# Second block of a two-block transformer: the projection products become one stream that is put out between the stages of the attention items

## The chip, the cores and the metric

The kernel runs on one core of a Trainium2 chip. All weights and activations are float32; every large matrix product is made as three products of "fp32r" parts (high by high, low by high, high by low). The metric is the device time of one execution in microseconds (us), and the less the better.

## The reference, cut to what matters

512 tokens of width 1024 pass through a first block (two layers of mixer and feed-forward network) and a second block. The change is in the second block, which computes:

```python
h = rmsnorm(x, attn_norm)
z = h @ w_in                                    # 3*512 columns dil, 3*512 columns fox, 8 forget gates
o_dil = dilated_attention(q_d, k_d, v_d, rel_bias)       # 8 heads of 64, causal, a bias by distance
log_f = log_sigmoid(z_forget + b_forget)
c = cumsum(log_f, axis=1)
s = q_f @ k_f.T * 64 ** -0.5 + c[t] - c[s]               # fox: 8 heads of 64, causal
o_fox = softmax(s) @ v_f
x = x + concat(rmsnorm(o_dil, g_dil), rmsnorm(o_fox, g_fox)) @ w_out
x = x + hierarchical_moe(rmsnorm(x, ffn_norm))           # 1 of 4 groups, 2 of its 8 experts
```

## The kernel before

Tokens stand in four tiles of 128. A weight "unit" of 2048 floats a partition is loaded into a `raw` tile (SyncE's queue), ScalarE (ACT) rounds it to `whi` (L147), VectorE (DVE) makes `wlo` (L148), and `mm3` (L171 to L173) issues the three products of one 128x512 piece. There are three buffers each of `raw`, `whi` and `wlo`. The order of instructions on each engine is chosen by a scheduler when the kernel is built; an engine then takes them strictly in that order.

Around the change the program runs so. The last feed-forward network of the first block ends with its down products; token tile by token tile follow the post norm, the residual and the pre norm of the second block (`rq`, `hn`), transposes on TensorE (L197) and copies to `acth` and `actl` (L201, L202): these are `h`. Then `second` runs:

1. `qkv` for dil: `nat_proj` makes `sv` (v, 96 products), then the forget product (24 products) and its chain in `forget` (DVE and ACT: exp, log, reciprocal, running sum, `fc` last), then q and k of all eight heads (192 products, kept as `sq`, `skh`, `skl`).
2. `attend` for dil: 16 items (4 pairs of heads by 4 query tiles), each with three stages that `staged` interleaves by `LAG = (0, 1, 2)`: `scores` (L1013, L1016, then `soft`: DVE adds the bias and takes the maximum at L882, POOL negates it at L883, ACT takes exp at L884), `turn` (transposes L893, copies `pt`), `values` (L913). After a pair's last tile `back` (L922) turns the output to tokens on partitions.
3. `out_norm` of dil: norm, transposes, copies to `mixd`.
4. the same for fox: 288 products, then 16 items with a mask product (L1019), and two decay products a pair (L1115), which read `fc`.
5. `tail`: `out_proj` with all of `w_out` (192 products, first the left 512 columns for the four tiles, then the right ones), and per tile the residual, norm and router. Then `moe`, whose 32 experts are read from memory.

`self.hold`, set from `HOLD_D` and `HOLD_F`, keeps the splitting of some later weights behind earlier instructions. The line numbers of the changed kernel are some two higher up to `back`, and its scores, masks, decay products stand at L1105 and L1111, L1108, L1160.

Of the kernel before, what the change touches and what calls it, by code (L numbers as in the profile page):

```python
# [22 lines left out]
P = 128  # L23
# [66 lines left out]
class Builder:  # L90
# [60 lines left out]
    def col_unit(self, w, c0, n=256):  # L151
        """w [1024, N]: all rows, n columns -> views [P, 8, n]"""
# [9 lines left out]
    def row_unit(self, w, r0, c0=0, n=1024, raw=None):  # L162
        """rows r0.. of w, n columns: [P, 2048/n, n]"""
# [25 lines left out]
    def to_T(self, src, tt, dst, kb0=0, n=None):  # L189
        """src [P tok, n*128] fp32 -> dst (hi, lo) tiles [:, kb0.., tt block]"""  # L190
# [14 lines left out]
    def mean_sq(self, ss, j, src, q=None):  # L205
        """ss[:, j] = sum(src ** 2) / D over half a row"""
# [127 lines left out]
    # ---- even mixer  # L334
    def even(self, h, mix):
# [17 lines left out]
        # v, tokens on partitions  # L353
# [22 lines left out]
        # masked, transposed token weights: wm[s, g, t], s <= t  # L376
# [7 lines left out]
        # a and u, transposed  # L384
# [103 lines left out]
    def nat_proj(self, w, c0, n, h):  # L488
        """h^T w[:, c0:c0+n] with tokens on partitions: four PSUM tiles"""
# [13 lines left out]
    def odd_tables(self):  # L503
        """rotary tables; kept for the odd mixer"""
# [14 lines left out]
    def odd_ret(self, h, mb):  # L519
        """retention, two heads at a time; returns what is left to emit"""  # L520
# [10 lines left out]
        def two(c0, c1):  # L531
            """columns c0..c0+255 and c1..c1+255 side by side, tokens on partitions"""
# [101 lines left out]
    def nsa(self, np_, cp, h, mixp, mid):  # L634
# [15 lines left out]
        def rope(pool, n, a, b, tt):  # L650
            """rotates the first 16 columns of each 64 in n viewed [P, a, b, 64]"""
# [11 lines left out]
        # kc | vc | ks | vs  # L663
# [23 lines left out]
        # kw | vw | gates  # L687
# [15 lines left out]
        # compressed keys and values  # L703
# [22 lines left out]
        # q: head b and head b + 4 share a block of 128 rows  # L726
# [87 lines left out]
        def selected(qt, br, b):  # L814
            """heads b and b + 4 over the selected keys (br 0) or the window's (br 1)"""
# [56 lines left out]
    def soft(self, pool, s, bias, nk, acc):  # L872
        """one head, one tile of queries: scores in PSUM (plus bias from SBUF) -> exp(s - max), the sums into acc"""
# [14 lines left out]
    def keys_first(self, pool, e, nk, odd):  # L888
        """e [queries, keys] -> keys on partitions, block by block"""
# [11 lines left out]
    def staged(self, items, lag=LAG):  # L901
        """items' stages interleaved: an item's stage k is put out lag[k] items after its first"""
# [6 lines left out]
    def pair_av(self, av, et, qt, v):  # L909
        """v^T e of two heads, one in each half of av's rows"""  # L910
# [5 lines left out]
    def back(self, pool, av, tag):  # L916
        """av, features on partitions -> tokens on partitions, block by block, in PSUM"""
# [50 lines left out]
    def qkv(self, pool, w, c0, h, between=None):  # L968
        nc = self.nc
        q = self.t(pool, "sq", [P, 8, T], F32R)  # L970
        kh = self.t(pool, "skh", [P, 8, T], F32R)
        kl = self.t(pool, "skl", [P, 4, T], F32R)
        v = self.t(pool, "sv", [P, NT, 512])
        pv = self.nat_proj(w, c0 + 1024, 512, h)
        for tt in range(NT):
            nc.scalar.activation(v[:, tt, :], pv[tt], AF.Copy)
        if between:
            between()
        for which in range(2):
            for b in range(2):  # L980
                u = self.col_unit(w, c0 + which * 512 + b * 256)
                for f in range(2):
                    p = self.ps()
                    for k in range(KD):
                        self.mm3(p, [z[:, k, f * P:(f + 1) * P] for z in u], [z[:, k, :] for z in h], k == 0,
                                 k == KD - 1)
                    for i in range(2):
                        hd = 4 * b + 2 * f + i
# [735 lines left out]
```

## Time and profile before

| | us |
|---|---|
| three timed runs | 1931.82, 1935.98, 1929.04 (median 1931.82) |
| the profiled execution, span from its first to its last instruction | 1934.0 |
| TensorE busy with products | 1866.0 (96 %) |
| TensorE busy loading weights | 1485.9 (77 %) |
| DVE, ACT, POOL busy | 1075.0, 789.2, 165.9 |
| mean granted TensorE clock | 0.971 of full speed |

The profiled execution is known by its span alone, and that is its own time here; it lies 2.2 us above the median of the timed runs. Products overlap in TensorE's pipeline, so a row's duration is longer than the distance to the next start: the starts tell the rate.

### The profile page before, as it was taken

How to read it: one execution, taken by the hardware profiler on the slowest of the kernel's cores; microseconds unless marked ns; L12 is line 12 of the kernel's file. 1: busy time of each engine (PE TensorE's matmuls, PEld its weight loads, DVE VectorE, ACT ScalarE, POOL GpSimd, SP SyncE). 2: the span in 40 equal slices, each digit the busy share in tenths (PEclk: the TensorE clock that was granted, in tenths of full speed). 3: DMA queues.
4: the chain of work that ended last, by engine and by line, in shares of the span. 5: the costliest groups of instructions: out<-in, count | busy, mean ns of one | idle time of the engine just before them, and what ended most of it. 6: DMA issues, size and time to landing. Idle time of an engine off the chain costs nothing.

```text
span 1934.0 us, 24404 instructions
## 1 busy us (share of the span) xinstructions
PE 1866.0 (96%) x9690; PEld 1485.9 (77%) x9691; DVE 1075.0 (56%) x1677; ACT 789.2 (41%) x1282; POOL 165.9 (9%) x303
## 2 busy tenths in 40 slices
PE   8999999999999989999999999999999979999997
PEld 6778888888899777678888888776686767676774
DVE  7654535444753444645444445663524477788876
ACT  6343222222422434644222222444536337666664
POOL 1010000000332100011000000200201240000000
PEclk9999999999999996999999999997998979999999
DMA  7433232323331210053233232240211408899994
GB/s 226 142 131 131 88 109 88 109 87 107 122 97 47 87 44 1 1 174 109 87 97 100 89 108 88 88 147 15 90 61 50 145 1 284 305 328 301 314 315 186
DMA packets 178326, 246.56 MB, mean 127 GB/s; under 512 B 10838, under 2 KB 144886, under 8 KB 178082
## 3 DMA queue, kind: packets, MB, share of 16 engines
q1 hardware_dynamic: 168352, 230.31, 36.0%
q10 hardware_dynamic: 9858, 14.67, 2.3%
q8 instruction: 77, 1.26, 0.3%
q14 instruction: 39, 0.32, 0.1%
HBM read 238.65 MB, written 8.93 MB: 128 GB/s over the span
## 4 chain that ended last, share of the span: by engine, by line
PE 29%; issue 19%; DVE 3%; POOL 2%; ACT 2%; POOLq 0%; ACTq 0%; DVEq 0%
PE mm L1408 6%; PE mm L1429 3%; PE px L1447 3%; PE px L1248 3%; PE mm L172 3%; PE mm L173 3%; PE mm L171 3%; PE px L913 2%; PE tp L893 1%; PE mm L1013 1%; PE mm L1016 1%; POOL rq L213 0%; DVE wlo L148 0%; ACT whi L147 0%; PE tp L1372 0%
## 5 line engine op out<-in xcount | busy, mean ns | idle before, releaser
L148 DVE TENSOR_TENSOR wlo<-raw,whi 128x2048 fp32r<-128x2048 f32 (+2 forms) x175 | 397.1, 2271 | 296.0 <-ACT whi L147 295.5
L147 ACT ACTIVATE whi<-raw 128x2048 fp32r<-128x2048 f32 (+2 forms) x175 | 331.6, 1897 | 476.1 <-issue 198.2
L171 PE MATMUL mm<-acth,whi 128*128 128x512 f32 (+2 forms) x968 | 365.6, 378 | 0.0
L172 PE MATMUL mm<-actl,whi 128*128 128x512 f32 (+2 forms) x968 | 364.7, 377 | 0.0
L173 PE MATMUL mm<-acth,wlo 128*128 128x512 f32 (+2 forms) x968 | 364.3, 376 | 0.0
L172 PEld LDWEIGHTS mm<-actl,whi 128*128 128x128 f32 (+1 forms) x968 | 181.9, 188 | 34.5 <-issue 1.0
L171 PEld LDWEIGHTS mm<-acth,whi 128*128 128x128 f32 (+1 forms) x968 | 181.9, 188 | 34.2 <-issue 0.7
L173 PEld LDWEIGHTS mm<-acth,wlo 128*128 128x128 f32 (+1 forms) x968 | 181.8, 188 | 34.2 <-issue 0.2
L171 PE MATMUL mm<-whi,acth 128*128 128x256 f32 (+2 forms) x480 | 159.9, 335 | 2.1 <-ACT gate L693 1.7
L172 PE MATMUL mm<-wlo,acth 128*128 128x256 f32 (+2 forms) x480 | 158.1, 330 | 0.6 <-DVE wlo L148 0.6
L173 PE MATMUL mm<-whi,actl 128*128 128x256 f32 (+2 forms) x448 | 145.4, 326 | 0.4 <-DVE actl L202 0.3
L317 DVE TENSOR_TENSOR macc<-px,macc 128x512 f32<-128x512 f32 x144 | 97.7, 689 | 75.2 <-PE px L173 75.2
L171 PE MATMUL px<-whi,hidh 128*128 128x512 f32 x352 | 137.5, 391 | 0.6 <-DVE macc L317 0.6
L173 PE MATMUL px<-whi,hidl 128*128 128x512 f32 x352 | 137.9, 392 | 0.0
L172 PE MATMUL px<-wlo,hidh 128*128 128x512 f32 x352 | 137.4, 390 | 0.0
L1408 PE MATMUL mm<-wlo,hg 128*128 128x512 f32 x256 | 102.3, 403 | 2.1 <-DVE wlo L148 2.1
L1408 PE MATMUL mm<-whi,hg 128*128 128x512 f32 x256 | 102.5, 401 | 0.0
L171 PEld LDWEIGHTS mm<-whi,acth 128*128 128x128 f32 x480 | 91.5, 191 | 11.1 <-ACT gate L693 1.9
L172 PEld LDWEIGHTS mm<-wlo,acth 128*128 128x128 f32 x480 | 91.4, 191 | 8.7 <-DVE wlo L148 1.5
L173 PEld LDWEIGHTS mm<-whi,actl 128*128 128x128 f32 x448 | 85.4, 191 | 6.9 <-DVE actl L202 1.0
L297 DVE TENSOR_TENSOR hidf<-mm,silu 128x512 f32<-128x512 f32 x44 | 30.4, 691 | 94.8 <-PE mm L173 94.8
L171 PEld LDWEIGHTS px<-whi,hidh 128*128 128x128 f32 x352 | 66.1, 188 | 16.3 <-DVE macc L317 1.5
(408 smaller groups left out, 2816.8 us busy)
## 6 DMA issues: line engine op xcount, KB each, us to landing
raw<-in_w_expert_gate SPq DMA_DIRECT2D x64, 512.0 KB, 5.7
raw<-in_w_expert_up SPq DMA_DIRECT2D x64, 512.0 KB, 8.4
actl<-in_w_expert_down SPq DMA_DIRECT2D x30, 1024.0 KB, 7.1
raw<-in_ffn_w_gate SPq DMA_DIRECT2D x22, 1024.0 KB, 5.3
raw<-in_ffn_w_up SPq DMA_DIRECT2D x22, 1024.0 KB, 5.3
raw<-in_ffn_w_down SPq DMA_DIRECT2D x22, 1024.0 KB, 4.8
raw<-in_od_w_in SPq DMA_DIRECT2D x12, 1024.0 KB, 5.1
raw<-in_w_in SPq DMA_DIRECT2D x12, 1024.0 KB, 5.3
```

Of the source, the lines that this page charges most:

```text
L147: self.nc.scalar.activation(hi[:, :n], raw[:, :n], AF.Copy)
L148: self.nc.vector.tensor_tensor(lo[:, :n], raw[:, :n], hi[:, :n].bitcast(F32), op=ALU.subtract)
L171: mm(out, l[0], r[0], start=first, stop=False)
L172: mm(out, l[0], r[1], start=False, stop=False)
L173: mm(out, l[1], r[0], start=False, stop=last)
L297: nc.vector.tensor_tensor(hf, pu[f], s, op=ALU.mult)
L317: nc.vector.tensor_tensor(m, p, m, op=ALU.add)
L913: self.nc.tensor.matmul(av[64 * i:64 * i + 64], v(i, kb), et[i][:, kb * P:(kb + 1) * P], start=kb == 0, stop=kb == qt)
L1248: self.nc.tensor.matmul(o, h2[i][:, tt, kb * P:(kb + 1) * P], s1[:, tt, :], start=tt == 0 and i == 0, stop=tt == NT - 1 and i == 1)
L1408: nc.tensor.matmul(ps, hg[kb][:, ee, :], hl[i][:, k, :], start=kb == 0 and i == 0, stop=kb == KD - 1 and i == 1)
L1429: nc.tensor.matmul(dn[hf][64 * e:64 * e + 64, :], heT[:, f * P + 64 * e:f * P + 64 * e + 64], rv[e][:, f, hf * 512:(hf + 1) * 512], start= ...
L1447: nc.tensor.matmul(p, ST[i][:, tt * P:(tt + 1) * P], z, start=n == 0, stop=n == 3)
```

## The change

The projection products are written as pieces, each a generator that gives up control after three products (a "chunk"): v of dil (32 chunks), four pairs of dil (16 each: q and k of two heads), v of fox, pair 0 of fox, forget (8), pairs 1 to 3 of fox, and then the first half of the output projection (rows 0 to 511 of `w_out`, 32 chunks, added to `x`). The 32 items of both attentions are one list. TensorE's order is kept as written there (`manual_schedule`): v of dil and pair 0, then per slot `scores(n)`, `values(n-2)`, `turn(n-1)`, late pieces (`back`, the dil norm), and 7 chunks (5 from slot 16 on). Other engines' order is still chosen by the scheduler. The PSUM pools are closed and opened anew twice (`psum`): at the start of `second` and at the start of `tail`. `tail` keeps only rows 512 to 1023 of `w_out` (`second_out`, 96 products, tile by tile). The holds go; `x` moves to the tile of `actl`, the experts' down weights to that of `mixd`; a pair's weights are loaded by two transfers instead of a unit by one.

```diff
-HOLD_N, HOLD_D, HOLD_F = 8, 8, 8
+HOLD_N = 8
+QUOTA = (7, 5)
...
-    def qkv(self, pool, w, c0, h, between=None):
...
+    def pair_unit(self, w, c0):
+        raw = self.load_unit([(j * 1024, KD, P, w[:, c0 + 512 * j:c0 + 512 * j + P].rearrange("(k p) n -> p k n", p=P))
+                              for j in range(2)])
+        return [z.rearrange("p (w k n) -> p w k n", w=2, k=KD) for z in self.split_w(raw)]
+    def pair_piece(self, pool, w, c0, b, h, sets):
...
+            for which in range(2):
+                p = self.ps()
+                for k in range(KD):
+                    self.mm3(p, [z[:, which, k, :] for z in u], [z[:, k, :] for z in h], k == 0, k == KD - 1)
+                    if k < KD - 1:
+                        yield
...
+    @staticmethod
+    def stream(pieces):
+        ready = pieces[0][0]()
+        for n, (_, run) in enumerate(pieces):
+            now = ready
+            ready = pieces[n + 1][0]() if n + 1 < len(pieces) else None
+            yield from run(now)
...
-    def second(self, h, src=None):
+    def second(self, h, src):
...
+        self.psum(mm=3, sc=2, tp=2, px=1)
...
-        dq = self.qkv(qp, w, 0, h, lambda: fg.extend(self.forget(qp, w, h)))
...
-        self.attend(at, dq, toep, False, o)
-        out_norm(o, "out_norm_dil_2", mix[0])
-        self.hold = self.marks[-HOLD_D]
-        fq = self.qkv(qp, w, 1536, h)
-        self.hold = ()
...
+        dense = self.stream([self.value_piece(qp, w, 1024, h, vals[0])] + [pair(0, b) for b in range(4)]
+                            + [self.value_piece(qp, w, 2560, h, vals[1]), pair(1, 0), self.forget_piece(qp, w, h, fg)]
+                            + [pair(1, b) for b in range(1, 4)]
+                            + [(lambda: None, lambda _: room()), self.half_out_piece(A["w_out_2"][0], mix[0])])
...
+        until(lambda: vals[0] and sets[0])
...
+        with self.tc.manual_schedule(engines={mybir.EngineType.PE}):
+            for n in range(len(items) + 2):
+                if n < len(items):
...
+                    until(lambda: len(sets[a]) > b and (a == 0 or fg))
+                    built[n] = self.item(at, b, qt, sets[a], vals[a], (toep, decay)[a], a == 1, o[a], S)
+                    built[n][0]()
+                if n >= 2:
...
+                    built[n - 2][2]()
...
+                if 1 <= n <= len(items):
+                    built[n - 1][1]()
+                for f in late.pop(n, []):
+                    f()
+                pull(QUOTA[n >= 16])
...
+        for tt in range(NT):
+            self.to_T(out_norm(tt, o[1], g), tt, mix[1])
...
-        self.out_proj(A["w_out_2"][0], mix, part, (normed, routed), (0, 1))
+        self.second_out(A["w_out_2"][0], mix, part, (normed, routed))
```

On TensorE, at the start of the second block, the order before puts v products (`mm`, of tiles 0 and 1) ahead of the transposes of token tile 2 (`tp` from `hn`); 24 of them stand there, and 20 more ahead of the transposes of tile 3:

```order
L173 MATMUL mm_9835<-whi_9818,actl_9580 128x512
L171 MATMUL mm_9835<-whi_9818,acth_9579 128x512
L172 MATMUL mm_9835<-wlo_9819,acth_9579 128x512
L173 MATMUL mm_9835<-whi_9818,actl_9580 128x512
L197 MATMUL tp_9745<-ident_72,hn_9735 128x128 x4
L197 MATMUL tp_9753<-ident_72,hn_9735 128x128 x4
L171 MATMUL mm_9822<-whi_9876,acth_9579 128x512
L171 MATMUL mm_9848<-whi_9818,acth_9579 128x512
```

In the changed kernel the same place reads:

```order
L173 MATMUL px_9705<-whi_9519,hidh_9397 128x512
L174 MATMUL px_9705<-wlo_9520,hidh_9397 128x512
L175 MATMUL px_9705<-whi_9519,hidl_9398 128x512
L199 MATMUL tp_9745<-ident_72,hn_9735 128x128 x4
L199 MATMUL tp_9753<-ident_72,hn_9735 128x128 x4
L199 MATMUL tp_9786<-ident_72,hn_9776 128x128 x4
L199 MATMUL tp_9794<-ident_72,hn_9776 128x128 x4
L173 MATMUL mm_9839<-whi_9821,acth_9579 128x512
```

The last down products (`px`) are followed by all 16 transposes of tiles 2 and 3, and no v product stands ahead of these any more.

On ACT, ahead of the first scores, the changed kernel puts the rounding of the third pair's weights (`whi_10169`, which takes the buffer that pair 0's products read) ahead of the copies of pair 0's keys (`skh`), which the first scores read; on DVE `wlo` and `skl` stand in the same order:

```order
L149 ACTIVATE whi_10016<-raw_10013 128x2048
L960 ACTIVATE sq_9950<-mm_9953 64x512 x2
L149 ACTIVATE whi_10169<-raw_10166 128x2048
L960 ACTIVATE skh_9951<-mm_9982 64x512
L963 ACTIVATE skh_9951<-mm_9982 64x512
L960 ACTIVATE skh_9951<-mm_9982 64x512
L963 ACTIVATE skh_9951<-mm_9982 64x512
```

In the kernel before all eight heads' keys are made ahead of the first scores, so pair 0's stand long ahead.

On DVE, at slots 13 to 15, the forget chain (`raw` 8x512, ending in `fc`) now stands among the soft maxima, copies and splits of the stream:

```order
L1045 RECIPROCAL raw_10982<-raw_10982 8x512
L150 TENSOR_TENSOR wlo_11006<-raw_11002,whi_11005 128x2048
L1046 TENSOR_TENSOR raw_10982<-raw_10982 8x512
L968 SCALAR_TENSOR_TENSOR sq_11009<-mm_11012,sq_11009 64x512
L1047 TENSOR_TENSOR raw_10982<-raw_10982 8x512
L1049 MEMSET raw_10982 8x512
L1048 SCALAR_TENSOR_TENSOR raw_10982<-raw_10982 8x512
L968 SCALAR_TENSOR_TENSOR sq_11009<-mm_11012,sq_11009 64x512
L1050 SCALAR_TENSOR_TENSOR raw_10982<-raw_10982 8x512
L150 TENSOR_TENSOR wlo_11202<-raw_11198,whi_11201 128x2048
L1053 CAST fc_10995<-raw_10982 8x512
L1054 TENSOR_TENSOR fc_10995<-raw_10982,fc_10995 8x512
```

On TensorE the decay products that read `fc` (L1160) stand behind the last forget product with 27 products of the stream, the scores, values and turn of slot 15 between; before, q and k of dil, all of the dil attention and 288 products lay between. At the end of the second block, after the last `back`, the 16 transposes of the fox norm follow with no product between them; before, products of the first half of the output projection stood there.

## Rows read from the trace of the kernel before

**Rows 1.** The page, parts 1, 2 and 5: busy time, slices, costly groups.

```profile
PE 1866.0 (96%) x9690; PEld 1485.9 (77%) x9691; DVE 1075.0 (56%) x1677; ACT 789.2 (41%) x1282; POOL 165.9 (9%) x303
PEclk9999999999999996999999999997998979999999
L147 ACT ACTIVATE whi<-raw 128x2048 fp32r<-128x2048 f32 (+2 forms) x175 | 331.6, 1897 | 476.1 <-issue 198.2
```

**Rows 2.** Windows: length, busy PE, PEld, DVE, ACT, POOL; clock; DMA.

```profile
1263.00:1323.00 60.00, 60.00 (x264) 47.26 (x265) 30.92 (x35) 25.99 (x33) 0.00 (x0) 1.00 0.28 89
1327.00:1348.00 21.00, 20.94 (x78) 12.73 (x78) 6.54 (x23) 8.98 (x30) 1.66 (x8) 0.51 0.08 25
1384.00:1393.00 9.00, 6.39 (x35) 4.67 (x32) 4.86 (x7) 3.76 (x10) 4.66 (x8) 1.00 0.41 130
1453.50:1471.00 17.50, 17.50 (x68) 10.20 (x67) 6.17 (x22) 7.85 (x26) 1.66 (x8) 0.51 0.16 67
1480.40:1491.30 10.90, 10.90 (x91) 7.42 (x90) 6.13 (x23) 7.54 (x24) 1.66 (x8) 1.00 0.01 2
1539.00:1596.00 57.00, 44.05 (x238) 38.43 (x236) 41.90 (x143) 22.27 (x48) 24.62 (x36) 0.82 0.01 2
1596.00:1934.00 338.00, 323.00 (x1641) 230.92 (x1641) 260.55 (x325) 211.41 (x264) 4.24 (x9) 0.99 0.85 291
```

**Rows 3.** Timeline of PE, start of block: start, duration, line, what.

```profile
1249.58 0.39 PE L171 MATMUL mm<-whi,acth 128*128 128x512 f32 x1
...
1262.99 0.50 PE L171 MATMUL mm<-whi,acth 128*128 128x512 f32 x1
```

**Rows 4.** Timeline of DVE, the norm chain at that start.

```profile
1251.59 2.28 DVE L148 TENSOR_TENSOR wlo<-raw,whi 128x2048 fp32r<-128x2048 f32 x1
...
1259.04 0.21 DVE L148 TENSOR_TENSOR wlo<-raw,whi 128x64 fp32r<-128x64 f32 x1
```

**Rows 5.** Groups of ACT, 1263 to 1330: busy, mean ns, idle before.

```profile
L961 ACT ACTIVATE skh<-mm 64x512 fp32r<-64x512 f32 x8 | 4.7, 592 | 0.1
```

**Rows 6.** Groups of DVE, the same stretch.

```profile
L962 DVE TENSOR_TENSOR skl<-mm,skh 64x512 fp32r<-64x512 f32 x8 | 5.5, 688 | 13.9 <-ACT skh L961 13.9
```

**Rows 7.** Timeline of DVE, forget chain, first to last.

```profile
1280.42 0.74 DVE L1054 TENSOR_SCALAR fx<-mm,bf 8x512 f32<-8x512 f32 x1 [0.81 <-PE mm L173]
...
1287.56 3.34 DVE L1061 RECIPROCAL fa<-fa 8x512 f32<-8x512 f32 x1 [2.04 <-ACT fe L1060]
...
1299.37 0.68 DVE L1070 TENSOR_TENSOR fc<-fd,fc 8x512 fp32r<-8x512 f32 x1
```

**Rows 8.** Groups of PE in one fox pair, 1480.4 to 1491.3.

```profile
L1019 PE MATMUL mm<-cmask,identb 128*128 128x128 bf16 x8 | 1.1, 225 | 0.0
...
L1115 PE MATMUL mm<-fc,sel 40*128 40x512 f32 x2 | 0.7, 438 | 0.0
```

**Rows 9.** Timeline of PE, last items, fox norm, output projection.

```profile
1500.52 0.55 PE L893 MATMUL tp<-ident,pe 128*128 128x128 f32 x3 [1.48 <-ACT pt L898]
...
1510.68 0.60 PE L922 MATMUL px<-ident,nat 128*128 128x128 f32 x4
...
1520.64 0.48 PE L172 MATMUL mm<-wlo,mixd 128*128 128x512 f32 x1
1520.95 0.39 PE L173 MATMUL mm<-whi,mixd 128*128 128x512 f32 x1
...
1538.88 0.39 PE L171 MATMUL mm<-whi,mixd 128*128 128x512 f32 x1
```

**Rows 10.** Timeline of DVE, the last fox items.

```profile
1497.10 2.29 DVE L148 TENSOR_TENSOR wlo<-raw,whi 128x2048 fp32r<-128x2048 f32 x1
```

**Rows 11.** Timeline of POOL, the same place.

```profile
1496.86 0.21 POOL L883 TENSOR_SCALAR nm<-mx 128x1 f32<-128x1 f32 x1 [2.47 <-ACT nat L919]
1497.34 2.11 POOL L883 TENSOR_SCALAR nm<-mx 128x1 f32<-128x1 f32 x1 [0.27 <-DVE mx L882]
```

**Rows 12.** Timeline of ACT, the same place.

```profile
1499.49 0.61 ACT L884 ACTIVATE pe<-pe,nm 128x384 f32<-128x384 f32 x1 [1.68 <-POOL nm L883]
```

More of the change, by code (lines that the diff above doesn't have):

```diff
@@ L966, in stack @@
             nc.vector.scalar_tensor_tensor(dst_h[o], src, scale, hv, op0=ALU.mult, op1=ALU.subtract)
-    def qkv(self, pool, w, c0, h, between=None):
[L969 to L988, printed above, removed]
-                        r = slice(64 * i, 64 * i + 64)
-                        if which == 0:
-                            self.stack(q[:, hd, :], None, p[r], r, 0.125)
-                        else:
-                            self.stack(kh[:, hd, :], kl[:, hd // 2, :], p[r], r, both=True)
-        return q, kh, kl, v
@@ L1014, in scores @@
                 for i in range(2):
                     r = slice(64 * i, 64 * i + 64)
-                    nc.tensor.matmul(ps[i][:, :nk], q[r, 2 * b + i, qs], kl[r, b, 0:nk], start=False, stop=not mask)
-                if mask:
-                    for i in range(2):
-                        nc.tensor.matmul(ps[i][:, nk - P:nk], self.identb, self.cmask, start=False, stop=True)
-                st["e"] = [self.soft(pool, ps[i], bt[i](nk), nk, sums[:, qt, i:i + 1]) for i in range(2)]
-            def turn():
-                st["et"] = [self.keys_first(pool, st["e"][i], nk, i) for i in range(2)]
@@ L1077, in second, with value_piece, prep, run @@
-    def second(self, h, src=None):
+                    if which == 0:
+                        self.stack(q[:, i, :], None, p[r], r, 0.125)
+                    else:
+                        self.stack(kh[:, i, :], kl, p[r], r, both=True)
+                yield
+            sets.append((q, kh, kl))
+        return prep, run
+    def value_piece(self, pool, w, c0, h, box):
+        def prep():
+            return [self.row_unit(w, kh * 512, c0, 512) for kh in range(2)]
+        def run(u):
+            v = self.t(pool, "sv", [P, NT, 512], bufs=2)
+            for tt in range(NT):
+                p = self.ps()
+                for kb in range(KD):
+                    self.mm3(p, [z[:, kb, tt * P:(tt + 1) * P] for z in h], [z[:, kb % 4, :] for z in u[kb // 4]], kb == 0,
+                             kb == KD - 1)
+                    if kb < KD - 1:
+                        yield
+                self.nc.scalar.activation(v[:, tt, :], p, AF.Copy)
+                yield
+            box.append(v)
+        return prep, run
@@ new lines, in half_out_piece, with prep, run @@
+    def half_out_piece(self, w, act):
+        def prep():
+            return [self.row_unit(w, 0, 512 * hf, 512) for hf in range(2)]
+        def run(u):
+            for tt in range(NT):
+                for hf in range(2):
+                    p = self.ps()
+                    for k in range(4):
+                        self.mm3(p, [a[:, k, tt * P:(tt + 1) * P] for a in act], [z[:, k, :] for z in u[hf]], k == 0, k == 3)
+                        if k < 3:
+                            yield
+                    xs = self.x[:, tt, HALF[hf]]
+                    self.nc.vector.tensor_tensor(xs, p, xs, op=ALU.add)
+                    yield
+        return prep, run
@@ new lines, in pull, with until, at_slot @@
+        def pull(n):
+            for _ in range(n):
+                next(dense, None)
+        def until(done):
+            while not done():
+                next(dense)
+        until(lambda: vals[0] and sets[0])
+        items = []
+        for a in range(2):
+            o.append(None)
+            S = {}
+            for b in range(4):
+                for qt in range(NT):
+                    items.append((a, b, qt, S))
+        built = {}
+        late = {}
+        def at_slot(n, f):
+            late.setdefault(n, []).append(f)
@@ L1249, in send, with second_out, tail @@
                                       stop=tt == NT - 1 and i == 1)
-    def tail(self, mix, src):
+    def second_out(self, w, act, part, finish):
+        un = [self.row_unit(w, 512, 512 * hf, 512) for hf in range(2)]
+        for tt in range(NT):
+            for hf in range(2):
+                p = self.ps()
+                for k in range(4):
+                    self.mm3(p, [a[:, k, tt * P:(tt + 1) * P] for a in act], [z[:, k, :] for z in un[hf]], k == 0, k == 3)
+                if tt:
+                    finish[hf](tt - 1)
+                part(tt, hf, p)
+        for f in finish:
+            f(NT - 1)
+    def tail(self, mix):
         nc, A = self.nc, self.A
@@ L1320, in tail @@
         self.done(self.bp)
+        self.moe(h2, st, s1, first)
         self.done(self.mixd)
[L1322 to L1323 removed]
         most = nc.values_load(st["cnt"][0:1, NE:NE + 1], min_val=0, max_val=T)
```

213 lines of the change are left out of this document (128 added, 85 removed).

## The prediction

> **What bounds the kernel now.** I first read the page: TensorE is busy with products for 96 % of the span, and loads weights for 77 % [rows 1]. Products overlap, so the first figure cannot show what an idle or slowed TensorE costs; the windows can. Three kinds of stretch stand behind the end of the first block.
>
> - Dense products: 264 in 60.0 us at full clock, 0.227 us each [rows 2].
> - The two attentions and their norms. The granted clock is 0.51, that is 1.2 GHz in place of 2.4, from 1327 to 1348 and from 1453.5 to 1471. These 38.5 us hold work worth 19.6 us, so 18.9 us go to the clock. Ahead of each drop TensorE had gone over from dense products to the short products of the items. In the dil norm TensorE is busy 6.39 of 9.0 us [rows 2].
> - From 1539 to 1596 the routing chain on DVE, ACT and POOL, and from 1596 on the experts, with the DMA engines at 0.85 and 291 GB/s [rows 2]. The change adds nothing to either, so what it gains or loses by the first tile of the last half of the output projection stays to the end. If the experts' transfers could start earlier for a late chain, some would be hidden; with three `raw` buffers the prefetch is full long before (0.01 of DMA share from 1539 to 1596), so I count nothing.
>
> So the sum runs from the last down product of the first block, 1249.6 [rows 3], to the end of that tile, 1538.9 [rows 9]: 289.3 us before.
>
> **The change part by part.** The number of products is the same in this stretch: 288 for each attention, 24 for forget, 96 for one half of the output projection and 24 for one tile of the other, 720 by 0.227 = 163.4 us. (Before, the halves are columns, after, they are rows; a tile of the rest is 24 products either way.) What changes is what else stands there.
>
> 1. Start. Before, 45 v products (24, 20 and 1) run while the norms of tiles 2 and 3 are made, from 1249.58 to 1262.99 [rows 3]. After, all transposes of these tiles stand ahead of the first v product, since the reopened PSUM pools put whatever uses the old ones first. The same norm chain then lies bare: 13.4 us. One more thing is late: before, a small split of 0.21 us stood between tile 2's copies and tile 3's norm, now a full one of 2.28 [rows 4], 2.1 more. Its neighbours wait for POOL and ACT too, so I take 0.5 of it: 13.9 us, with 13.4 and 15.5 as the ends.
> 2. Attention. A pair of fox takes 10.9 us at full clock [rows 2]; of it 1.1 are mask and 0.7 decay products [rows 8], which dil has not: 9.1. Four of each: 80.0 us. All half-clock time is taken as gone here, since dense products now stand in each slot; restarts come under 6.
> 3. Changing between kinds. The first dense product behind transposes takes 0.31 us to the next start, not 0.23 [rows 9]: 0.08, twice in each of the 31 slots that have dense work: 5.3 us.
> 4. First scores. Pair 0's keys are ready only when ACT has rounded the third pair's weights (1.90 us [rows 1]; it waits for pair 0's last product, whose buffer it takes), then copied keys four times (0.59 each [rows 5]), while DVE splits (2.28) and then makes `skl` twice (0.69 each [rows 6]). 1.90 + 2.28 + 1.38 = 5.6, less three products of cover, 0.7: 4.9 us. Queued behind it are all scores. If DVE took `skl` first it would be 1.90 + 2.36 + 0.69 - 0.7 = 4.3; the low end is 2.4, the copies alone.
> 5. Forget. Its chain took 1280.42 to 1300.05, 19.6 us, before [rows 7], under q and k of dil, and nobody read `fc` until fox. After, the first decay product of fox waits for it and all of fox's items stand behind that product. The cover is 27 products (6.1 us) and one item (10.9 / 4 = 2.7, less a little): 8.6 us. The chain is much the same in the new place: two soft maxima come in, the two splits that stood in it before still do. I take 20.0, so 11.4 us bare, with 8 and 15 as the ends.
> 6. Restarts at half clock behind the four bare stretches (start, first scores, forget, end). No row shows what a restart into dense products costs; the two falls above cost 8.6 and 10.3 us each where items alone followed. Here dense products follow, so nearer to nothing: 2 us each, 8 us, with 0 and 34 as the ends.
> 7. The dil norm: its 16 transposes remain, four groups of 0.4 us, 1.6 us; its waits of 2.6 us go, since chunks stand between.
> 8. End. No dense product is left for the last three slots, and the fox norm has none between its transposes. Before, the last `back` began at 1510.68 and products went on from 1520.64 [rows 9], with 20 products (4.5 us) in that gap. After, the gap is bare: 9.96, plus copies of the last tile (0.59 and 0.69), less 0.4 of `back` itself (under 2) = 10.8, and the wait for the last exp, 1.48 in the row [rows 9], now without a filler: 12.3 us. The 96 products of the first half were brought forward into the slots for it.
> 9. Waits within the stream. At 1497.10 a split took DVE 2.29 us [rows 10]; POOL's `nm`, else 0.21, took 2.11 beside it [rows 11]; exp waited 1.68 for it [rows 12], and TensorE 1.48 for what followed [rows 9]. The stream brings about eleven such splits among the items. A slot holds 7 or 5 chunks, 4.8 or 3.4 us of products, between scores and turn, so most of these delays are covered: I take 4 us, with 0 and 11 by 1.48 = 16 as the ends.
>
> The loads of the pairs (two of half the size each), the move of `x` and of the down weights, and the holds are costed at nothing: the DMA engines are at 0.28 and less in the dense stretch [rows 2] and dense products hide them; with that cover gone one load would be late by a few us, within 9.
>
> Sum: 163.4 + 13.9 + 80.0 + 5.3 + 4.9 + 11.4 + 8 + 1.6 + 12.3 + 4 = 304.8 us, 15.5 more than 289.3. The profiled span of 1934.0 becomes 1949.5; it lies 2.2 above the median of the runs, 1931.82, so the time is 1947.3.
>
> **The rivals.**
>
> A, the stream pays, faster. The mechanism is interleaving alone: the chains of 4 and 5 run under the chunks, as each had cover before, and no split delays a turn. For it: in the trace every one of these chains is hidden where dense products lie beside it. Against: TensorE's order is fixed, and chunks behind a waiting product can't move ahead. Without 4, 5, 9 and six of the eight us in 6 the sum is 278.5, 10.8 less than before: 1921. It decides where the wait ahead of the first decay product is under about 1 us and first scores wait under 1. The Trainium skill, "Perfetto Trace Analysis", section "Optimization Strategy", says that a kernel with several regimes may gain when they are interleaved; the half-clock stretches of items next to dense stretches agree that there is something to interleave, and by that rule alone this rival would be the forecast.
>
> B, the splits hold up the soft maxima, clearly slower. If each of the eleven delays shows in full and restarts cost 4 us each, 12 + 8 come on top: 1967. For it: the rows at 1497. Against: 3.4 to 4.8 us of cover in each slot. It decides where TensorE idles over 1 us in most slots. The Trainium skill, "SBUF — State Buffer", section "Who interferes with whom", says that a DVE instruction with two SBUF inputs contends with a GpSimd instruction that reads SBUF, and that the other one is blocked; the 2.11 us of `nm` within the 2.29 us of the split agree.
>
> C, no change. Forget's chain is hidden, because it starts earlier or is shorter than in the trace, and the rest stands: 304.8 - 11.4 - 2 = 291.4, 2.1 more, 1934.
>
> **How the numbers follow.** Forecast 0.48, A 0.21, B 0.15, C 0.16. Faster or slower begins at 0.3 % here, 5.8 us, about what the measurement tells from no change. C lies within it with most of its chance, and so does a little of A: faster 0.21, same 0.15, slower 0.64. The forecast's own range is 1938 to 1957, by the ends of 1, 4, 5 and 9. The range of 8 in 10 reaches into A and B: 1924 to 1962.
>
> **What would show it.** In the profile after: no v product until about 1263.5; an idle of some 5 us ahead of the first scores and of some 11 ahead of the first decay product; a clock near 1.0 in the middle of the items; about 10 us with little on TensorE between the last `back` and the next dense product; the routing chain at 57 us and the experts at 338, as before. It is wrong if `fc` is ready when the decay product comes, if half clock goes on inside the items in spite of the chunks (then some 19 us more), or if the experts' stretch becomes shorter because transfers start ahead of it.

## The result, and the profile after

The changed kernel took 1956.35 us (median of four runs, 1953.1 to 1961.49), the kernel before 1932.41 us beside it: a ratio of 1.0128, 95 % interval 1.0103 to 1.0154. It is slower by about 24 us; 15.5 were forecast. The profiled span is 1955.1 us against 1934.0.

The page of the changed kernel, parts 1 and 2 (beside [rows 1]):

```profile
PE 1848.4 (95%) x9690; PEld 1483.7 (76%) x9691; DVE 1080.0 (55%) x1685; ACT 789.2 (40%) x1282; POOL 158.8 (8%) x303
...
PEclk9999999999999988999999999889989878999999
```

TensorE is busy for 17.6 us less in a span that is 21.1 longer: it waits. Where it does, the view of waits of TensorE tells, from 1249 to 1620 (what waited, for what, us in total, times, longest):

```profile
PE mm L1160 <- DVE fc L1054: 12.9, 1, 12.9
PE tp L199 <- DVE hn L228: 10.8, 2, 5.8
PE tp L199 <- ACT pt L900: 5.3, 4, 2.6
PE sc L1105 <- ACT skh L963: 4.9, 2, 2.6
...
PE tp L199 <- DVE pe L1170: 3.7, 2, 3.3
PE mm L1160 <- ACT g L1162: 2.9, 1, 2.9
...
PE tp L199 <- DVE acth L204: 2.4, 1, 2.4
```

The first row is the decay product that waits for the forget chain, the second the norms at the start of the block, the fourth the first scores: three of the four bare stretches of the prediction. The fifth and the last belong to the fourth of them, the end. The third row is the dil norm's transposes, whose waits the prediction had said would go (step 7); the sixth, a later decay product, it did not have.

I measure the same stretch as the prediction's sum: from the end of the last down product to the end of the 720th dense product behind it. Idle is its length less TensorE's busy time. The loss to half clock is the busy time by one minus the granted clock, summed over windows of 2 us. The rest is work.

| us | stretch | idle | half clock | rest |
|---|---|---|---|---|
| before | 289.3 | 9.1 | 18.7 | 261.5 |
| changed | 311.3 | 46.3 | 16.7 | 248.2 |

So the work itself became 13.3 us shorter, and 37 us more of idle stand against that. Counted from each product's start to the next, without the waits and weighted by the granted clock, the items' products took 80.5 us in place of 93.2, the dense products 167.1 in place of 168.4; why the items cost less, no run shows. The half clock did not go: it moved from the items to five restarts, that is, stretches at half clock that begin in a wait and last beyond it. They stand at the start, the first scores, `fc`, the decay product of the sixth row and the end; cut where the clock changes, 3.2, 3.7, 3.6, 2.9 and 3.6 us are lost there. Not every wait had a restart: behind those of 2.6 and 1.8 us at the dil norm, between 1471 and 1484, the clock stayed full. Windows of the changed kernel (columns as in [rows 2]) show the waits and the restarts:

```profile
1247.04:1261.51 14.47, 3.69 (x18) 3.20 (x17) 11.93 (x14) 7.49 (x15) 7.13 (x6) 0.63 0.76 235
1296.07:1303.00 6.93, 1.99 (x6) 1.14 (x4) 3.88 (x4) 5.01 (x6) 0.00 (x0) 0.68 0.27 72
1414.40:1427.80 13.40, 0.63 (x3) 0.19 (x1) 13.19 (x12) 4.35 (x4) 0.00 (x0) 0.64 0.24 78
1427.80:1434.00 6.20, 6.04 (x29) 4.70 (x30) 0.92 (x6) 3.85 (x8) 0.41 (x2) 0.50 0.92 337
1435.20:1489.60 54.40, 46.88 (x286) 35.42 (x284) 27.44 (x58) 30.50 (x69) 5.99 (x22) 1.00 0.18 56
1488.00:1496.00 8.00, 5.30 (x28) 4.22 (x29) 4.18 (x7) 4.83 (x8) 0.38 (x2) 0.61 0.65 254
1540.50:1551.10 10.60, 4.45 (x20) 3.47 (x21) 5.20 (x10) 4.24 (x12) 5.52 (x12) 0.68 0.38 101
1551.10:1558.30 7.20, 7.20 (x27) 5.79 (x26) 2.07 (x3) 1.45 (x4) 0.00 (x0) 0.76 0.02 5
```

From 1414.4 DVE is busy for 13.19 of 13.4 us and TensorE for 0.63; then TensorE works for 6.2 us at 0.50, half clock. What DVE does there is the forget chain, and within it, in the order that the scheduler chose, two splits of the stream and two copies of queries (0.68 and 0.69 us), which the chain waits behind (timeline of DVE):

```profile
1414.11 3.34 DVE L1045 RECIPROCAL raw<-raw 8x512 f32<-8x512 f32 x1 [1.74 <-ACT raw L1044]
1417.38 2.22 DVE L150 TENSOR_TENSOR wlo<-raw,whi 128x2048 fp32r<-128x2048 f32 x1
...
1424.60 2.25 DVE L150 TENSOR_TENSOR wlo<-raw,whi 128x2048 fp32r<-128x2048 f32 x1
...
1427.23 0.68 DVE L1054 TENSOR_TENSOR fc<-raw,fc 8x512 fp32r<-8x512 f32 x1
```

No run held these two splits behind the chain; they are 4.5 of its 21.3 us. The other parts of the program moved little: from the end of the stretch to the experts' first product 58.7 us (57.7 before), from there to the end 338.3 (337.6).

The timeline of TensorE in the changed kernel, at the start, behind the first scores and at the decay product:

```profile
1252.99 1.94 PE L199 MATMUL tp<-ident,hn 128*128 128x128 f32 x8 [5.79 <-DVE hn L228]
1259.91 1.94 PE L199 MATMUL tp<-ident,hn 128*128 128x128 f32 x8 [4.99 <-DVE hn L228]
1261.51 0.78 PE L173 MATMUL mm<-whi,acth 128*128 128x512 f32 x1
...
1304.45 0.63 PE L173 MATMUL mm<-acth,whi 128*128 128x512 f32 x1
1304.88 0.63 PE L174 MATMUL mm<-actl,whi 128*128 128x512 f32 x1
...
1427.96 1.22 PE L1160 MATMUL mm<-fc,sel 40*128 40x512 f32 x2 [12.93 <-DVE fc L1054]
```

Before, v products filled the first place [rows 3].

### The profile page after: what moved, and what is told of

It reads as the page before. It is cut to its first block, busy times and chain, and to the rows that moved or that the text cites. A ratio compares the mean times of both kernels' runs of the same rounds, so it can differ in the third digit from the quotient of the medians.

```text
span 1955.1 us, 24407 instructions
## 1 busy us (share of the span) xinstructions
PE 1848.4 (95%) x9690; PEld 1483.7 (76%) x9691; DVE 1080.0 (55%) x1685; ACT 789.2 (40%) x1282; POOL 158.8 (8%) x303
## 3 DMA queue, kind: packets, MB, share of 16 engines
q1 hardware_dynamic: 176672, 230.31, 35.4%
## 5 line engine op out<-in xcount | busy, mean ns | idle before, releaser
L150 DVE TENSOR_TENSOR wlo<-raw,whi 128x2048 fp32r<-128x2048 f32 (+1 forms) x175 | 397.4, 2273 | 317.8 <-ACT whi L149 314.8
L149 ACT ACTIVATE whi<-raw 128x2048 fp32r<-128x2048 f32 (+1 forms) x175 | 331.6, 1896 | 474.4 <-PE mm L174 195.4
L175 PEld LDWEIGHTS mm<-acth,wlo 128*128 128x128 f32 (+1 forms) x968 | 182.4, 188 | 34.6 <-issue 0.2
```

The source lines that it names most:

```text
L149: self.nc.scalar.activation(hi[:, :n], raw[:, :n], AF.Copy)
L150: self.nc.vector.tensor_tensor(lo[:, :n], raw[:, :n], hi[:, :n].bitcast(F32), op=ALU.subtract)
L175: mm(out, l[1], r[0], start=False, stop=last)
```

## The experiments

All times are beside runs of the kernel before on the same chip. Over the twelve runs and the two kernels the last down product ended anywhere from 1241.5 to 1252.6 us, with nothing changed ahead of it; so stretches are compared, each from one trace, and the ratios for the whole.

**Forget early.** The forget piece goes to the second place of the stream.

```diff
-        dense = self.stream([self.value_piece(qp, w, 1024, h, vals[0])] + [pair(0, b) for b in range(4)]
-                            + [self.value_piece(qp, w, 2560, h, vals[1]), pair(1, 0), self.forget_piece(qp, w, h, fg)]
-                            + [pair(1, b) for b in range(1, 4)]
+        dense = self.stream([self.value_piece(qp, w, 1024, h, vals[0]), self.forget_piece(qp, w, h, fg)]
+                            + [pair(0, b) for b in range(4)] + [self.value_piece(qp, w, 2560, h, vals[1])]
+                            + [pair(1, b) for b in range(4)]
```

> The forget piece stands second in the stream, behind v of dil and ahead of all pairs, so that its chain runs under pair 0's products and the first slots; nothing else is changed. Theory (each bare chain has its own price): the wait of 12.9 us ahead of the first decay product goes, and some 2 us of half clock behind it, so the time falls by 13 to 16 us against the changed kernel, to about 1942; the wait ahead of the first scores (4.9) may grow by up to 2, since one more split stands ahead of the keys. Rival (DVE and ACT are behind at that place anyway, so that the wait moves to the next item): the decay product's wait goes but waits at the next scores and turns take most of it, and the time falls by less than 5 us.

Measured: 1957.75 us, ratio 1.0123 (1.0097 to 1.0149); stretch 311.9, idle 41.4, half clock 22.3. The largest wait of the kernel was taken away, and the time stayed. View of waits of this kernel, TensorE:

```profile
PE tp L199 <- DVE hn L228: 10.1, 3, 5.8
PE sc L1105 <- ACT skh L963: 7.5, 1, 7.5
PE tp L199 <- ACT pt L900: 6.9, 3, 3.2
PE mm L1160 <- ACT g L1162: 5.3, 3, 2.4
...
PE px L915 <- ACT pt L900: 2.3, 2, 1.8
```

The row on `fc` is gone. First scores grew from 4.9 to 7.5, the norm's transposes from 5.3 to 6.9, decay products from 2.9 to 5.3, and values wait 2.3: 8.9 us came back as waits, and 5.6 as half clock behind them. My theory that each bare chain has its own price fell here; the rival was right.

**One pool.** The layout of before stays; scores, values and decay products take other tags.

```diff
-        self.psum(mm=3, sc=2, tp=2, px=1)
...
-            ps = [self.ps("sc") for _ in range(2)]
+            ps = [self.ps("px") for _ in range(2)]
...
-                S[b] += (self.ps("px"),)
+                S[b] += (self.ps(),)
...
-            p = self.ps()
+            p = self.ps("tp")
...
-        self.psum(mm=4, tp=2, px=2)
```

> The PSUM pools are not opened anew: the layout of before (4 mm, 2 tp, 2 px) stays throughout, scores use px, a pair's values use mm, decay products use tp; the stream is the same. In the order 34 and 23 products (down and v) stand ahead of the transposes of tiles 2 and 3 again. Theory (the reopened pool lays the norm chain bare): the first v product follows the last down product at once, the stretch up to dense work loses some 10 us and the restart 1.3, so the time falls by 10 to 12 us against the changed kernel, to about 1945. Rival (the start is only where the wait shows; with the products used up there, the first scores or the first slots wait instead): under 5 us. A wait of turns for tp buffers held by decay products would take back up to 2 us.

Measured: 1939.13 us, ratio 1.0036 (1.0020 to 1.0051); stretch 291.3, idle 33.5, half clock 8.6. The stretch is 20.0 us less than in the changed kernel, more than the theory's 10 to 12: idle fell by 12.8 and half clock by 8.1. Waits of this kernel:

```profile
PE tp L1159 <- DVE fc L1054: 13.0, 1, 13.0
...
PE tp L199 <- DVE hn L228: 1.4, 2, 1.0
PE tp L895 <- ACT g L1161: 1.1, 1, 1.1
```

The norms at the start are covered again (10.8 us to 1.4), and the second decay product of a pair no longer waits 2.9 us for the last of three `mm` buffers. The two traces, cut at the same dense products, say where the 20.0 us went:

| up to the end of dense product | changed | one pool |
|---|---|---|
| 100: the start | 38.6 | 26.7 |
| 260: first scores | 55.0 | 55.1 |
| 500: `fc` | 99.5 | 99.6 |
| 600: the dil norm | 46.3 | 46.3 |
| 680: the decay product that waited 2.9 | 39.9 | 35.4 |
| 720: the end | 31.9 | 28.2 |

So 11.9 us are from the start, 4.5 from the decay product and 3.7 from the end; elsewhere the traces agree to 0.1 us. The prediction and the theory had not seen the last: the pools were reopened at the start of `tail` as well, and in the changed kernel the first products of the last half of the output projection stand behind all 16 transposes of the fox norm. With one pool they pass eight of these (timeline of TensorE):

```profile
1525.45 0.78 PE L173 MATMUL mm<-whi,acth 128*128 128x512 f32 x1
...
1528.16 0.66 PE L199 MATMUL tp<-ident,pe 128*128 128x128 f32 x4 [0.17 <-DVE acth L204]
```

**Late pieces behind the chunks.**

```diff
-                for f in late.pop(n, []):
-                    f()
                 pull(QUOTA[n >= 16])
+                for f in late.pop(n, []):
+                    f()
```

> Late pieces (back, the dil norm's transposes) stand behind the slot's chunks and no longer between turn and chunks; nothing else is changed. The trace of the changed kernel has waits of 0.38, 0.50, 2.62 and 1.78 us ahead of the dil norm's transposes and some 0.3 ahead of each back, each put down to ACT's copies of turned exponentials (pt), which free the two tp buffers. Theory (the two tp buffers are the cause): these waits go, since the copies run under the chunks: 5 to 7 us less than the changed kernel, about 1950. Rival (the norm's own chain through ACT, POOL and DVE is late): the waits stay at about 5 us, now behind the chunks.

Measured: 1944.8 us, ratio 1.0060 (1.0041 to 1.0079); stretch 300.6, idle 39.0, half clock 14.7: 10.7 us less, of which 7.3 are idle; the theory's 5 to 7 had idle alone. The waits of the dil norm's transposes are gone from the list (5.3 us before), and those ahead of each `back`. In the changed kernel the cause can be read off ACT and TensorE (timelines):

```profile
1472.46 0.62 ACT L886 ACTIVATE pe<-pe,nm 128x384 f32<-128x384 f32 x1 [2.04 <-POOL nm L885]
...
1473.79 0.38 ACT L900 ACTIVATE pt<-tp 128x256 f32<-128x256 f32 x1
```

```profile
1470.95 0.66 PE L895 MATMUL tp<-ident,pe 128*128 128x128 f32 x4
1474.23 0.66 PE L199 MATMUL tp<-ident,pe 128*128 128x128 f32 x4 [2.62 <-ACT pt L900]
```

Two turns fill both `tp` buffers at 1470.95. The copy that frees one stands on ACT behind the exponentials of the next item, at 1473.79, and the norm's transposes, which stand directly behind the turns, wait for it, and all chunks behind them. A decay product still waits 2.7 us in this run, now for a key's `skl`.

**Keys first.** The splits of the third pair's weights are held until pair 0's keys are made.

```diff
-            nc.scalar.activation(dst_h[o], src, AF.Copy, scale=scale)
-            nc.vector.tensor_tensor(dst_l[r], src, hv, op=ALU.subtract)
+            ka = nc.scalar.activation(dst_h[o], src, AF.Copy, scale=scale)
+            self.keys = (ka, nc.vector.tensor_tensor(dst_l[r], src, hv, op=ALU.subtract))
...
         def prep():
-            return self.pair_unit(w, c0 + b * P)
+            if c0 == 0 and b == 2:
+                self.hold = self.keys
+            u = self.pair_unit(w, c0 + b * P)
+            self.hold = ()
+            return u
```

> The splitting of the third pair's weights is held until pair 0's keys are copied; nothing else is changed. Theory: the wait ahead of the first scores, 2.36 and 2.58 us in the trace of the changed kernel, falls from 4.9 to about 2.5 us (four copies of 0.59, one skl, less three products); the time falls by 2 to 3 us, to about 1954, within what the timing can tell. Rival (keys are late for another reason, such as the switch of TensorE or the products' end): the wait stays at 4 to 5 us.

Measured: 1952.47 us, ratio 1.0090 (1.0066 to 1.0114); stretch 306.5, 4.8 us less. The wait of the first scores fell from 4.9 to 2.2 us, as the theory had it, and half clock by 2.5, which it had left out. By the whole time alone this edit is hardly told from none: its interval overlaps that of the changed kernel (1.0103 to 1.0154).

**The three together.** One pool, late pieces behind and keys first at once.

> The three edits that each gave time, together: pools not reopened, late pieces behind the chunks, keys ahead of the third pair's splits; forget stays where the change put it. The stretch from the last down product to the first tile of the last half of the output projection was 311.3 us in the changed kernel and 291.3, 300.6 and 306.5 with one edit each, so 20.0, 10.7 and 4.8 less. Theory (separate waits, prices add): 276 us, and about 1921 in all, less than the kernel before the change (289.3 and 1932). Rival (the chains on DVE and ACT are shared, a wait removed comes back at the next place, as it did when forget was moved): no better than the best of the three, about 290 and 1938.

Measured: 1928.64 us, ratio 0.9984 (0.9966 to 1.0002); stretch 282.4, idle 26.0, half clock 8.5. Of the 35.5 us that the three gave one by one 28.9 came together. The prices add for the most part, not wholly, and the rival's 290 is refuted. The forget chain is bare still, 12.2 us.

**The three, and forget early.**

> The same three edits, and forget second in the stream, ahead of all pairs. Alone that move took away 12.9 us of wait at the first decay product and gave all of it back (first scores 2.6 more, decay products 2.4, the norm's transposes 1.6, values 2.3, half clock 5.6). Theory (what gave it back were just the places that the three edits mend): 13 us of wait and 3 of half clock less than with the three edits alone, about 260 us and 1905 in all. Rival (the chain delays the first scores on DVE whatever stands around it): first scores wait 5 us or more, and less than half of it is gained.

Measured: 1917.47 us, ratio 0.9928 (0.9903 to 0.9952); stretch 271.1, idle 19.1, half clock 3.8. The move that alone gave nothing gives 11.3 us here. First scores wait, as the rival said, but it costs less than half. DVE and TensorE of this kernel at that place (timelines):

```profile
1286.26 1.21 DVE L1054 TENSOR_TENSOR_SCAN raw<-raw 8x512 f32<-8x512 f32 x1
1287.50 0.68 DVE L964 TENSOR_TENSOR skl<-mm,skh 64x512 fp32r<-64x512 f32 x1
```

```profile
1283.85 0.30 PE L1109 MATMUL px<-skh,sq 128*128 128x128 f32 x1 [0.74 <-DVE sq L968]
1289.47 0.48 PE L1109 MATMUL px<-skh,sq 128*128 128x128 f32 x1 [5.32 <-ACT skh L963]
```

The keys' `skl` stands behind the running sum of forget on DVE, ACT's next `skh` behind that, and the second scores product waits 5.32 us.

**The three, and forget in the middle of dil** (behind two pairs).

> The same three edits, and forget behind two pairs of dil, so that its chain runs on DVE among slots that already have items, away from the first scores, with over six slots until the first decay product. Theory: the wait at the first decay product goes and no wait takes its place, since each slot has 4.8 us of products as cover: 13 to 16 us less than with the three edits alone, about 1905. Rival (DVE in order: the soft maxima behind the 3.3 us reciprocal and the 2.3 us splits hold up turns): two or three waits of 2 us or more in slots 5 to 8, gain under 8 us.

Measured: 1920.67 us, ratio 0.9940 (0.9916 to 0.9963); stretch 275.8, idle 17.0, half clock 10.8. The gain is 6.6 us, under 8, as the rival said, but with one new wait and not two or three: values wait 3.5 us for a copy on DVE. A decay product waits 3.0 as it did with the three edits alone, and half clock is 2.3 more than without the move.

**Even slots**, 6 and 5 chunks in place of 7 and 5, with forget in the middle:

```diff
-QUOTA = (7, 5)
+QUOTA = (6, 5)
```

> As the last, with 6 chunks a slot for the first 16 slots and 5 then, so that the stream reaches into the last slots, 31 to 33, which had none. Theory: the waits and the half clock of these three slots go, 3 to 5 us less than the last. Rival (6 chunks, 4.1 us, are too little cover in the first 16 slots): as much is lost there in waits of turns, no difference.

Measured: 1925.07 us, ratio 0.9962 (0.9946 to 0.9978); stretch 280.4, idle 20.1: 4.6 us worse. Waits of this kernel:

```profile
PE px L1109 <- ACT skh L963: 7.5, 5, 2.7
```

Scores now wait for keys at three items and not at one: with fewer chunks a slot a pair's products end closer ahead of the slot that needs them. The last product of fox's first pair starts 1.0 us ahead of fox's first decay product, at 1396.06, where with 7 chunks it was 10.0. What is lost, then, is the lead of the keys; neither theory nor rival had named that.

**Which of the edits lets forget pay.** Two runs, with forget early and only one other edit.

> Two edits: pools not reopened (decay products in tp, so no wait for a third mm buffer), and forget second in the stream. With the pools alone the stretch from the last down product to the first tile of the last half was 291.3 us; with all three edits the move of forget gave 11.3 us, with none of them it gave nothing. Theory P (the move paid only once decay products no longer waited for an mm buffer): 280 us here, about 1927 in all. Theory N (it paid only once the late pieces were out of the way of turns): no gain here, about 291 us and 1939.

> Two edits: late pieces behind the chunks, and forget second in the stream; the pools are reopened as in the changed kernel. With the late pieces alone the stretch was 300.6 us. Theory N: 289 us here, about 1933 in all, and no waits of values or norm transposes for copies of pt. Theory P: no gain here, about 300 us and 1945, with 3 us or more of waits between decay products.

Measured: with one pool 1934.95 us, ratio 1.0009 (0.9989 to 1.0028), stretch 287.9, 3.4 less than without the move; with late pieces behind 1941.9 us, ratio 1.0055 (1.0034 to 1.0076), stretch 296.9, 3.7 less. Neither theory's 11 us came: by the stretch each edit lets about a third of the 11.3 us through. The whole times can't tell so little from nothing (1.0009 against 1.0036 with one pool alone, 1.0055 against 1.0060 with late pieces alone, the intervals overlap). In the first the norm's transposes take 8.1 us (5.3 with one pool alone), in the second decay products take 4.6, and in both the first scores take over 7 (4.9). Forget early with keys first alone was not run.

**More cover for the first scores.** Six chunks are pulled ahead of them.

```diff
         until(lambda: vals[0] and sets[0])
+        pull(6)
```

> The three edits and forget second, and six chunks (18 products) of pair 1 pulled ahead of the first scores. In the run without them the first scores waited 5.3 us for pair 0's keys, which stood behind the forget chain on DVE, and 2.6 us went to half clock behind it. Theory: 4.1 us of products cover most of it; 4 to 7 us less, a stretch of about 265 us and 1911 in all; the same chunks are missing at slots 29 and 30, which costs up to 2. Rival (scores simply come later, and the last slots lose as much): no difference.

Measured: 1920.41 us, ratio 0.9939 (0.9918 to 0.9959); stretch 271.9, idle 16.8, half clock 7.2. There is no difference, as the rival said, but not for its reason, the last slots. The wait of the first scores fell from 5.3 to 2.2 us; a turn waits 3.7 us elsewhere, and half clock is 3.4 more, of which 2.4 stand around that turn. There the chain of [rows 10] to [rows 12] is back, a split on DVE beside `nm` on POOL (timelines of DVE, POOL, ACT and TensorE):

```profile
1442.95 2.29 DVE L150 TENSOR_TENSOR wlo<-raw,whi 128x2048 fp32r<-128x2048 f32 x1
1443.12 2.19 POOL L885 TENSOR_SCALAR nm<-mx 128x1 f32<-128x1 f32 x1 [0.25 <-DVE mx L884]
1445.34 0.61 ACT L886 ACTIVATE pe<-pe,nm 128x384 f32<-128x384 f32 x1 [1.73 <-POOL nm L885]
1445.95 0.36 ACT L900 ACTIVATE pt<-tp 128x256 f32<-128x256 f32 x1
1446.37 0.69 PE L895 MATMUL tp<-ident,pe 128*128 128x128 f32 x2 [3.67 <-ACT pt L900]
```

**Chunks kept for the fox norm.** The same, 6 and 3 chunks a slot, and the rest between the norm's transposes.

```diff
-QUOTA = (7, 5)
+QUOTA = (6, 3)
...
+            pull(6)
+            for tt in range(NT):
+                self.to_T(out_norm(tt, o[1], g), tt, mix[1])
+                pull(2)
```

> The same, with 6 and 3 chunks a slot in place of 7 and 5, so that chunks are left for the fox norm: 6 of them behind the last back and 2 behind each tile's transposes, in TensorE's written order; what is left follows. Theory: 8 us of idle at the end go, about 258 us and 1904 in all. Rival (three chunks, 2.0 us, are too little cover for the soft maxima of the fox slots): turns and scores wait about 0.5 us in each of 18 slots, or half clock comes back there, and it is no faster than without.

Measured: 1914.38 us, ratio 0.9904 (0.9879 to 0.9929); stretch 269.4, idle 12.0, half clock 10.9. Waits of this kernel:

```profile
PE px L1109 <- ACT skh L963: 8.6, 5, 2.7
```

The fox norm's 4.2 us are gone from the list, but scores wait for keys at four items, as they did in the even run, and half clock is 3.7 more: 2.5 us are left of 8. The rival had half clock coming back, but no gain. The intervals of the two runs overlap a little. Of the kernels run this has the least time. Its interval overlaps that of the three with forget early; both beat the kernel before, by 1.0 and 0.7 %.

All stretches in one table, in us:

| kernel | stretch | idle | half clock | ratio to before |
|---|---|---|---|---|
| before | 289.3 | 9.1 | 18.7 | 1 |
| changed | 311.3 | 46.3 | 16.7 | 1.0128 |
| forget early | 311.9 | 41.4 | 22.3 | 1.0123 |
| one pool | 291.3 | 33.5 | 8.6 | 1.0036 |
| late pieces behind | 300.6 | 39.0 | 14.7 | 1.0060 |
| keys first | 306.5 | 43.7 | 14.2 | 1.0090 |
| the three | 282.4 | 26.0 | 8.5 | 0.9984 |
| three, forget early | 271.1 | 19.1 | 3.8 | 0.9928 |
| three, forget in the middle | 275.8 | 17.0 | 10.8 | 0.9940 |
| the same, even | 280.4 | 20.1 | 11.6 | 0.9962 |
| one pool, forget early | 287.9 | 27.2 | 11.4 | 1.0009 |
| late behind, forget early | 296.9 | 34.6 | 15.1 | 1.0055 |
| more cover | 271.9 | 16.8 | 7.2 | 0.9939 |
| more cover, fox norm filled | 269.4 | 12.0 | 10.9 | 0.9904 |

## Why the prediction was right, and where it was off

The forecast (slower, 1947 us, own range 1938 to 1957) came true with 1956.35, near its upper end. Of the 9.0 us that it was short, 6.5 lie in the stretch: the sum gave 304.8 us and 311.3 were measured. The rest is the first block, 2.5 shorter in the profiled execution, what follows the stretch, 1.7 longer, and the profiled execution itself: it was 2.2 us above the median in the kernel before, and it is 1.25 below it here. Step by step:

- Start (1), first scores (4) and forget (5) were found where they were put: 14.5 us against 13.9, 4.9 against 4.9, 12.9 against 11.4. The forget chain took 21.3 us in the new place, 1406.58 to 1427.91, not 20.0, with the two splits in it that the step expected.
- The end (8): from the last `back` to the next dense product 10.5 us (1540.57 to 1551.10) and 0.7 of wait ahead of it, 11.2 against 12.3. The size was right, but a part of it had another cause than the step gives: one pool takes 3.7 us of the end away.
- Waits within the stream (9) were mis-sized: 10.9 us against 4, within the ends of 0 to 16. The price lay well above the value taken, and the mechanism that the step named was not the one at work. The step put these waits down to splits that hold up POOL's `nm`. In the changed kernel the longest of 64 `nm` took 0.52 us, not 2.11 as in [rows 11], and none met a split. Whether they meet hangs on the order: with more cover four did, and one of them cost a turn 3.7 us. Step 7 fails here too: it let the dil norm's waits go, since chunks stand between, and the norm's transposes waited 5.3 us. What waited were these transposes for a `tp` buffer, decay products for an `mm` buffer (2.9), and the rest mostly by some 0.3 us at each `back`. With late pieces behind the chunks the first is gone; with decay products in `tp` the second is 1.1 with one pool, though 3.0 with the three edits. The prediction weighed engines and chains, and did not count the buffers of the new PSUM layout, though it is in the diff.
- Restarts at half clock (6) were mis-sized: 8 us against 13.6 (16.7 less about 3.1 that fall within the start and the end, which those steps hold). A restart cost 3.2 to 3.7 us and not 2: behind the wait for `fc` the clock was 0.50 for 6.2 us and more, half of which is lost. And a fifth, of 2.9 us, came with a wait of step 9, that of the decay product.
- Work (2, 3, 7 and the 720 products) was 243.3 us, which is what is left of 311.3 after the above, against 250.3. Most of this is the items, which in their written order cost less than a pair of [rows 2]: without the transposes of start and end their 80.5 us are about 76, where steps 2 and 7 have 81.6. This hid a part of the two errors.

In sum -7.0 + 5.6 + 6.9 + 1.5 + 0.6 - 1.1 = 6.5 us, the difference of 311.3 to 304.8.

The direction and the main mechanism, chains laid bare in a fixed order, were right; that the time fell within the own range is in part luck. Steps 6 and 9 were 12.5 us short, and 7.0 too many in the work made up for more than half of it. The range is not what its steps give either: the ends of 1, 4, 5 and 9 added up come to about 1937 and 1964, and it leaves out those of 6, the step with the widest ends (0 and 34).

Rival A (the stream pays) was the right picture of another kernel: with the pools left open, the late pieces behind the chunks, keys first and forget early the stretch is 271.1 us, 18 us less than before. Its points of decision were two, the waits ahead of the decay product and of the first scores. Forget early met the first alone, and the time stayed; and the three with forget early were faster with scores that still waited 5.3 us. The Trainium skill, "Perfetto Trace Analysis", section "Optimization Strategy", says that interleaving regimes may gain; by the runs it does here once the waits that the interleaving brought are out of the way. Rival B wanted TensorE idle for over 1 us in most slots; between the first scores and the last `back` there are six such waits in 32 items, and no `nm` met a split. Rival C (forget hidden, the rest as it is: 1934) fails on the wait of 12.9 us, and where forget early hid the chain, the time was 1957.75.

What stays open: why the items' products cost less in the written order; what the two splits within the forget chain cost, since no run moved them; and why some waits had a restart at half clock behind them and others of like length had none.

## What to carry to other kernels

When one engine's order is written by hand, every wait in it stops all work behind it, so the cover of each chain has to be counted in that order, the few buffers of a PSUM tag among the chains: who frees them, and behind what that engine does first. Taking away the largest wait alone may give nothing, where chains on the other engines then meet the next one. Reopening a pool is an edge in the order: nothing of the new may pass the last of the old, and a norm that was hidden lies bare.

## What the runs showed of the hardware that was not expected

A wait can cost more than its length. Behind a wait of 12.9 us TensorE's granted clock was 0.50 (1.2 GHz) for the next 6.2 us, though products were ready; behind 4.9 us of waits at the first scores dense products started 0.43 us apart for some 5 us, against 0.23 at 2.4 GHz. The Trainium skill, "TensorE: Matmul & The Clock Gate", section "HAM oscillation — how this bites in real kernels", describes, for a kernel that waits for DMA, that a wait for data that is long enough lets the next stretch start cold; the trace of the changed kernel agrees at five places, with 2.9 to 3.7 us lost at each. It was not so everywhere: behind waits of 2.6 and 1.8 us at the dil norm the clock stayed 1.00. The three edits and forget early took 27 us of idle away and 13 us of half clock with it.
